# Seven-part products moved from output blocks 2 to 5 to blocks 3 to 6, with all their weight sums on GpSimd

## The chip, the core and the metric

The kernel runs on one core of a Trainium2 chip. The profile calls the engines PE (TensorE, matrix products), DVE (VectorE), ACT (ScalarE), POOL (GpSimd) and SP (SyncE, which issues nearly all transfers from memory). The metric is the device time of one execution in microseconds; a kernel's time is the median of its runs. SBUF is the on-chip memory that engines read and transfers fill, PSUM holds the accumulators of the matrix products in eight banks of 128x512 float32.

## What is computed

One layer of a hybrid encoder for 256 tokens of width 4096: an input projection, two groups of heads, and an output projection with a normalised residual.

```
proj = einsum('bsd,dc->bsc', x, w_in)                  # w_in is 4096 x 16592
fox_out  = forgetting attention over 16 heads of 128
rwkv_out = RWKV-7 delta rule over 32 heads of 64, in chunks, with group norm
h   = concatenate([fox_out, rwkv_out]) * silu(z)
out = einsum('bsc,cd->bsd', h, w_out)                  # 4096 x 4096
x   = layernorm(ALPHA * x + out, ln_gain, ln_bias)
```

The change touches the output projection alone: `h` (256 x 4096) times `w_out` (4096 x 4096).

## The kernel before

**Precision.** Every float32 operand of a large product is split in two parts, a rounded high part and the rest. A product of a 128x128 piece of `h` with a 128x512 piece of weights is then three matmuls: high by high, low by high, high by low (`product`, lines 960, 961 and 963). The weights are split on the way: SP loads a tile of 128x1024 float32 (tag `wr`, four buffers, line 246), ACT writes the high part (line 148, names ending in `h`, four buffers) and DVE subtracts it to give the low part (line 149, names ending in `l`, three buffers). A tile holds two pieces, for two values of the contraction index `k`.

**Blocks and jobs.** The output projection has eight column blocks of 512. The list `plan` sets the order: a plain job `("n", b, q)` takes tile `q` of block `b`, that is `k = 2q` and `2q + 1`, for both halves of the tokens, so 4 products or 12 matmuls. `weights` keeps three jobs split ahead of the PE. Blocks 0 and 1 are done while the heads finish, 6 and 7 are plain.

**Seven-part products.** Blocks 2 and 3, and blocks 4 and 5, are done as pairs. For the six tiles in `FEW` (`q` from 6 to 11) of a pair, the 2 x 2 x 2 = 8 products of two token halves, two `k` and two blocks are replaced by seven (Winograd's form of Strassen's scheme). Call one such `q` a set. It needs sums of the left operand, which are made once for all pairs, and four sums of the weight tiles `one` (block `b`) and `two` (block `b + 1`) for each set:

- `combine_left(q)`: six GpSimd operations (lines 988 to 993) into a tile `sf`. `split_left(q)` then splits it (ACT line 999, DVE line 1000) into `sq` and over half of `h`'s own tile, and starts `combine_left(q + 2)`, since there are two buffers with the tag `t`.
- `combine("e1", b, q)`: GpSimd makes the first half of `ta` (line 277) and the first half of `tb` (line 278), DVE the second half of `ta` (line 281), GpSimd the second half of `tb` (line 282), which still reads tile `one`.

A set is four jobs: `e1` (two products, from tile `one`), `e2` (one, from half of tile `two`), `e3` (two, from `ta`) and `e4` (two, from `tb`), with two plain jobs between them. So a pair is six sets and 20 plain jobs.

**What sets the order around the change.** Each engine takes its instructions in the order in which they stand in its queue, and an instruction that waits holds up all behind it. A scheduler places them by the order of the calls; `tc.issue_after` and `tc.keep_in_program_order` fix some. Work on finished accumulators (`add`, `stats`, `gain`, and `merge` for the shared products) stands in the list `todo`, from which `drain(n)` takes n steps at a job. The left sums' splits of `split_left` stand in the same list. SP's queue holds the weight loads in the order of the jobs; a load waits until its `wr` buffer has been read for the last time.

## Time and profile before

| | |
|---|---|
| median of 3 runs | 1934.72 us (1933.67 to 1937.24) |
| the profiled execution, its own time | 1933.68 us |
| its span in the profile | 1931.9 us |
| PE busy in the span | 1903.4 us |
| block 2 begins on the PE, by the timeline | 1636.63 us |
| first pair ends, second ends, block 6 ends | 1740.72, 1830.44, 1873.96 us |

The kernel's time has 1.8 us outside the span. A matmul of 128x512 shows as about 0.39 us, but a new one begins every 0.23 us, since they overlap; so the PE is read by when matmuls begin and by the idle time ahead of one, not by the sum of their lengths. The rows of the timeline give the start, the duration, the engine, the line, the operation, result and operands, and in brackets the idle time before and what ended it. Tile names in the profile have no numbers of block and buffer: `wo_12l` is the low part of tile 12 of some block, `e_9l` the low part of a sum of set 9, `ta` and `tb` the weight sums, `sf` the left sums.

### The profile page before, as it was taken

What the parts mean: (1) busy time and instruction counts of PE and PEld (TensorE: products, weight loads), DVE (VectorE), ACT (ScalarE), POOL (GpSimd) and SP (SyncE); (2) the same over time, 40 slices, a digit from 0 to 9 for tenths busy, and PEclk for the clock granted to TensorE, in tenths of its full rate; (3) what the DMA queues carried; (4) which work ended last, traced back from release to release, by engine and by line L of the source; (5) the groups of instructions that cost most, each with busy time, mean ns of one, the idle gap of its engine ahead of it and who ended that gap; (6) DMA issues with size and microseconds to landing.
All of it is one profiled execution on the core that took longest, in us unless ns stands there. A gap on an engine that the chain in (4) does not pass through costs nothing.

```text
span 1931.9 us, 28208 instructions
## 1 busy us (share of the span) xinstructions
PE 1903.4 (99%) x9757; PEld 1578.9 (82%) x9757; DVE 1466.6 (76%) x2429; ACT 1007.7 (52%) x1577; POOL 358.8 (19%) x537
## 2 busy tenths in 40 slices
PE   9999999999999999999999999999999999899998
PEld 9887888888888888888888888888888888577786
DVE  7578768776877787678867786778677857789865
ACT  6554565446454645464556455645564555454543
POOL 0012102200220022012101310131013014733200
PEclk9999999999999999999999999999999999999999
DMA  9678766876687668767877787777777877456675
GB/s 345 179 209 227 213 199 220 235 224 193 205 245 221 199 202 253 212 198 219 236 202 214 217 231 200 222 218 223 205 222 224 288 226 229 142 193 211 212 227 182
DMA packets 271459, 421.37 MB, mean 218 GB/s; under 512 B 142482, under 2 KB 171300, under 8 KB 271316
## 3 DMA queue, kind: packets, MB, share of 16 engines
q1 hardware_dynamic: 271028, 419.23, 71.8%
q8 instruction: 76, 1.25, 0.3%
q14 instruction: 67, 0.55, 0.1%
q10 hardware_dynamic: 288, 0.34, 0.1%
HBM read 389.86 MB, written 29.64 MB: 217 GB/s over the span
## 4 chain that ended last, share of the span: by engine, by line
PE 93%; DVE 2%; POOL 2%; DMA 1%; issue 1%; ACT 0%; SPq 0%; DVEq 0%; POOLq 0%; ACTq 0%
PE acc L154 24%; PE acc L156 23%; PE acc L155 23%; PE oacc L963 5%; PE oacc L960 4%; PE oacc L961 4%; PE rh L706 1%; PE gp L592 1%; PE up L737 1%; PE sp L747 1%; PE accl L154 1%; PE accl L155 1%; PE accl L156 1%; DMA wo<-in_w_o_dram 1%; PE yp L769 0%
## 5 line engine op out<-in xcount | busy, mean ns | idle before, releaser
L821 POOL COPY pT<-lg 32x96 f32<-32x96 f32 x128 | 56.1, 438 | 632.9 <-DVE lg L817 628.2
L629 POOL COPY BKt<-BK 32x192 f32<-32x192 f32 x128 | 71.6, 559 | 62.5 <-DVE BK L626 57.5
L662 DVE TENSOR_REDUCE xc<-prod 128x8 f32<-128x16 f32 (+30 forms) x248 | 72.6, 293 | 6.6
L659 DVE TENSOR_TENSOR prod<-Nb,xc 128x8 f32<-128x8 f32 (+30 forms) x248 | 72.3, 291 | 3.0
L149 DVE TENSOR_TENSOR w_0l<-w,w_0h 128x1024 fp32r<-128x1024 f32 x31 | 38.6, 1245 | 37.6 <-ACT w_0h L148 28.5
L148 ACT CAST w_0h<-w 128x1024 fp32r<-128x1024 f32 x31 | 32.5, 1048 | 61.4 <-DMA w<-in_w_main_dram 43.0
L148 ACT CAST w_8h<-w 128x1024 fp32r<-128x1024 f32 x31 | 32.6, 1052 | 47.5 <-DMA w<-in_w_main_dram 21.8
L148 ACT CAST w_6h<-w 128x1024 fp32r<-128x1024 f32 x31 | 32.7, 1055 | 46.9 <-PE acc L155 35.3
L149 DVE TENSOR_TENSOR w_9l<-w,w_9h 128x1024 fp32r<-128x1024 f32 x31 | 38.0, 1225 | 23.0 <-issue 9.6
L149 DVE TENSOR_TENSOR w_11l<-w,w_11h 128x1024 fp32r<-128x1024 f32 x31 | 37.9, 1222 | 21.9 <-PE acc L156 16.2
L149 DVE TENSOR_TENSOR w_10l<-w,w_10h 128x1024 fp32r<-128x1024 f32 x31 | 37.9, 1223 | 19.9 <-PE acc L156 7.3
L149 DVE TENSOR_TENSOR w_15l<-w,w_15h 128x1024 fp32r<-128x1024 f32 x31 | 38.0, 1225 | 19.5 <-issue 16.6
L149 DVE TENSOR_TENSOR w_6l<-w,w_6h 128x1024 fp32r<-128x1024 f32 x31 | 38.9, 1253 | 16.1 <-ACT hry L780 10.3
L518 POOL COPY hr<-hr 32x16 f32<-32x16 f32 x64 | 45.4, 709 | 26.8 <-DVE hr L515 24.4
L154 PE MATMUL acc<-w_15h,x 128*128 128x512 f32 x124 | 50.2, 405 | 0.0
L154 PE MATMUL acc<-w_9h,x 128*128 128x512 f32 x124 | 50.0, 403 | 0.0
L148 ACT CAST w_10h<-w 128x1024 fp32r<-128x1024 f32 x31 | 32.6, 1052 | 32.9 <-DMA w<-in_w_main_dram 19.4
L156 PE MATMUL acc<-w_12l,x 128*128 128x512 f32 x124 | 48.5, 391 | 1.1 <-DVE w_12l L149 1.1
L154 PE MATMUL acc<-w_14h,x 128*128 128x512 f32 x124 | 49.5, 399 | 0.0
L149 DVE TENSOR_TENSOR w_7l<-w,w_7h 128x1024 fp32r<-128x1024 f32 x31 | 37.9, 1221 | 15.1 <-PE acc L156 13.1
L154 PE MATMUL acc<-w_0h,x 128*128 128x512 f32 x124 | 49.1, 396 | 0.0
L154 PE MATMUL acc<-w_1h,x 128*128 128x512 f32 x124 | 49.1, 396 | 0.0
(1058 smaller groups left out, 6821.1 us busy)
## 6 DMA issues: line engine op xcount, KB each, us to landing
w<-in_w_main_dram SPq DMA_DIRECT2D x496, 512.0 KB
wo<-in_w_o_dram SPq DMA_DIRECT2D x128, 512.0 KB
bt<-bk SPq DMA_DIRECT2D x88, 128.0 KB
Nb<-nd SPq DMA_DIRECT2D x16, 512.0 KB
hd<-hl SPq DMA_DIRECT2D x29, 256.0 KB
h<-hd SPq DMA_DIRECT2D x29, 256.0 KB
wr<-in_w_first_dram SPq DMA_DIRECT2D x15, 384.0 KB
lr<-in_w_lora_dram SPq DMA_DIRECT2D x15, 336.0 KB
```

The costliest lines, as they stand in the source:

```text
L148: latest[1] = nc.scalar.copy(hi[:, :n], src[:, :n])
L149: latest[0] = nc.vector.tensor_tensor(lo[:, :n], src[:, :n], hi[:, :n].bitcast(F32), ALU.subtract)
L154: nc.tensor.matmul(acc[:, :n], xs[k][:, 0, tt], hi[:, o : o + n], start=(k == 0), stop=False)
L155: nc.tensor.matmul(acc[:, :n], xs[k][:, 1, tt], hi[:, o : o + n], start=False, stop=False)
L156: nc.tensor.matmul(acc[:, :n], xs[k][:, 0, tt], lo[:, o : o + n], start=False, stop=(k == KT - 1))
L629: nc.gpsimd.tensor_copy(BKt[B * b : B * (b + 1), :, :, B * a : B * (a + 1)], BK[B * a : B * (a + 1), :, : NCH - 1, B * b : B * (b + 1)])
L659: first = nc.vector.tensor_tensor(prod[:, :, :, s + 1 :], nb[:, :, s : s + 1, s + 1 :].to_broadcast([P, 2, NJ, w]), xc[:, :, :, s + 1 :], ...
L662: solved = nc.vector.tensor_reduce(xc[:, :, :, s : s + 1], prod[:, :, :, s:], AX.X, ALU.add)
L821: (nc.gpsimd.tensor_copy if b % 2 else nc.scalar.copy)(pT[B * b : B * (b + 1), :, B * a : B * (a + 1)], lg[B * a : B * (a + 1), :, B * b : ...
L960: nc.tensor.matmul(acc, h, hi, start=n[0] == n[1], stop=False)
L961: nc.tensor.matmul(acc, l, hi, start=False, stop=False)
L963: nc.tensor.matmul(acc, h, lo, start=False, stop=not n[0])
```

## The change

The matmuls are the same in number. What moves:

- **The pairs** are now blocks 3 and 4, and blocks 5 and 6. Block 2 is a plain block between them and block 1, and takes the tiles in `FEW` first, since the left sums overwrite half of those rows of `h`.
- **The left sums.** `combine_left` for the first two sets stays behind block 0. All `split_left` calls, and the `combine_left` calls that they start, stand in `todo` of block 2, of which one step is taken at the jobs with `q` 0, 1, 3, 5 and 13, and one at the first job of block 3.
- **The weight sums** are four GpSimd operations in two jobs of their own, `t12` and `t34`; the DVE operation of line 281 is gone. `t12` comes a plain job and an `e4` earlier than `e1`.
- **Places apart.** The weight tiles of every second set (6, 8 and 10 of each pair) do not use `wr` buffers: `one` goes to a tile with the tag `lr` that is otherwise free, `two` in two halves to the part of `res` that belongs to block 7.
- **Accumulators of blocks 0 and 1** are added, measured and multiplied at once when the block ends, as six DVE operations in a row. Those of block 6 go to `todo`, as do the four `halves` steps, and are taken two at a job in block 7.
- Banks and the places of `load_tok` follow the new pairs.

```diff
-LEAD = (6, 4)
+PAIRS = {3: 3, 4: 3, 5: 5, 6: 5}
+LEAD = 4
...
+    plan += [("n", 2, q) for q in sorted(range(KT // 2), key=lambda q: q not in FEW)]
+    own_place = set()
+    for b in (3, 5):
         plain = [[(n, q) for q in range(KT // 2) if q not in FEW] for n in (b, b + 1)]
...
+        plan += [("n", *t) for t in lead[: LEAD - 2]]
+        for n, q in enumerate(FEW):
+            if n % 2 == 0:
+                own_place.add((b, q))
+            before = units[n - 1][1] if n else lead[-1]
+            plan += [] if n else [("n", *lead[-2])]
+            plan += [("t12", b, q), ("n", *before)] + ([("e4", b, FEW[n - 1])] if n else [])
+            plan += [("t34", b, q), ("e1", b, q), ("n", *units[n][0]), ("e2", b, q), ("e3", b, q)]
+        plan += [("n", *units[-1][1]), ("e4", b, FEW[-1])]
...
     def load():
         name, src = stream.pop()
+        b, q = [int(t) for t in name[2:].split("_")] if name[:2] == "wo" else (0, 0)
+        if b in PAIRS and (PAIRS[b], q) in own_place:
+            if b == PAIRS[b]:
+                raw = const.tile([P, 1024], F32, tag="lr", name=name)
+                nc.sync.dma_start(out=raw, in_=src.rearrange("p k c -> p (k c)"))
...
+            else:
+                apart[name] = [res[j][:, (NB - 1) * OB :] for j in range(2)]
+                for j in range(2):
+                    nc.sync.dma_start(out=apart[name][j], in_=src[:, j, :])
+            return
...
     def combine(kind, b, q):
...
+        g = nc.gpsimd.tensor_tensor
+        if kind[0] == "t":
+            t = sums_of[b, q, kind] = rpool.tile([P, 2 * OB], F32, tag="t", name=f"{kind}_{b}_{q}", bufs=2)
+            if kind == "t12":
+                g(t[:, :OB], b12, b11, ALU.subtract)
+                g(t[:, OB:], b22, t[:, :OB], ALU.subtract)
+            else:
+                g(t[:, :OB], b22, b12, ALU.subtract)
+                g(t[:, OB:], b21, sums_of[b, q, "t12"][:, OB:], ALU.subtract)
+            return
         if kind == "e1":
...
-            nc.gpsimd.tensor_tensor(t12[:, :OB], b12, b11, ALU.subtract)
-            nc.gpsimd.tensor_tensor(t34[:, :OB], b22, b12, ALU.subtract)
-            got = split(raws[one], 2 * OB, one)
-            with tc.issue_after(latest[0].ins):
-                nc.vector.tensor_tensor(t12[:, OB:], b22, t12[:, :OB], ALU.subtract)
-            nc.gpsimd.tensor_tensor(t34[:, OB:], b21, t12[:, OB:], ALU.subtract)
...
     def finished(b):
-        if b > 5:
+        if b < 2:
             with tc.issue_after(latest[0].ins):
-                for m in range(2):
-                    add(m, b)
-                for m in range(2):
-                    gain(m, b)
+                for step in (add, stats, gain):
+                    for m in range(2):
+                        step(m, b)
             return
...
+        if b == NB - 2:
+            todo.append(aggregate)
...
+            drain((2 if n <= LEAD or n > whole else 1) if kind == "n" else kind == "e4")
+        elif b > 1:
+            drain(2 if b == NB - 1 else q in (0, 1, 3, 5, 13))
...
+            if b == 1:
+                todo.extend(lambda q=q: split_left(q) for q in FEW)
+            elif b == 6:
+                todo.extend(lambda n=n: halves(n) for n in range(HALVED))
```

The built programs show the move in three places. The first is DVE's queue around set 8 of the second pair (blocks 4 and 5 before, 5 and 6 now). Before:

```order
L149 TENSOR_TENSOR wo4_8l_16890<-wo4_8_16835,wo4_8h_16889 128x1024
L281 TENSOR_TENSOR ta4_8_16885<-wo5_8_16847,ta4_8_16885 128x512
L1065 TENSOR_TENSOR res0_15796<-res0_15796,lg3_15993 128x512
L149 TENSOR_TENSOR wo4_12l_16911<-wo4_12_16873,wo4_12h_16910 128x1024
L1065 TENSOR_TENSOR res1_15797<-res1_15797,lg3_15993 128x512
L149 TENSOR_TENSOR wo5_8l_16924<-wo5_8_16847,wo5_8h_16923 128x512
L149 TENSOR_TENSOR e3_4_8l_16936<-ta4_8_16885,e3_4_8h_16935 128x1024
L149 TENSOR_TENSOR wo5_2l_16952<-wo5_2_16908,wo5_2h_16951 128x1024
L149 TENSOR_TENSOR e4_4_8l_16961<-tb4_8_16886,e4_4_8h_16960 128x1024
```

and with the change, where `e1`, `e2` and so on are the parts of a set:

```order
L150 TENSOR_TENSOR e1_5_8l_17206<-wo5_8_17122,e1_5_8h_17205 128x1024
L150 TENSOR_TENSOR wo5_12l_17222<-wo5_12_17138,wo5_12h_17221 128x1024
L150 TENSOR_TENSOR e2_5_8l_17234<-res1_15797,e2_5_8h_17233 128x512
L150 TENSOR_TENSOR e3_5_8l_17244<-t12_5_8_17168,e3_5_8h_17243 128x1024
L150 TENSOR_TENSOR wo6_2l_17263<-wo6_2_17231,wo6_2h_17262 128x1024
L150 TENSOR_TENSOR e4_5_8l_17272<-t34_5_8_17202,e4_5_8h_17271 128x1024
```

The sum `ta4_8`, which stood ahead of three splits, is gone from DVE, and so are the two steps of `gain` (L1065) in this set. The second place is SP's queue, the loads of the same sets, with the semaphores that each waits for. Before:

```order
L246 DMA wo4_8_16835<-in_w_o_dram 128x1024 [waits DMAHW5_49,Pool_49]
L937 DMA lg5_16725<-in_lng_dram 128x512 [waits DVE_49]
L246 DMA wo5_8_16847<-in_w_o_dram 128x1024 [waits DMAHW7_49,DMAHW3_49,DVE_49]
L246 DMA wo4_12_16873<-in_w_o_dram 128x1024 [waits DMAHW6_49,DMAHW4_49,DVE_49]
L246 DMA wo5_2_16908<-in_w_o_dram 128x1024 [waits DMAHW0_49,DVE_49]
L246 DMA wo4_9_16921<-in_w_o_dram 128x1024 [waits DMAHW1_49,Pool_49]
L246 DMA wo5_9_16933<-in_w_o_dram 128x1024 [waits DMAHW4_49,DVE_49]
```

and with the change, one set's loads further on:

```order
L266 DMA wo5_12_17138<-in_w_o_dram 128x1024 [waits DMAHW2_49,DVE_49,Pool_49]
L969 DMA lg7_17697<-in_lng_dram 128x512 [waits DMAHW3_49,DVE_49]
L266 DMA wo5_9_17150<-in_w_o_dram 128x1024 [waits DMAHW7_49,DVE_49]
L266 DMA wo6_9_17178<-in_w_o_dram 128x1024 [waits DMAHW5_49,DVE_49]
L365 DMA res0_15796<-in_xtok_dram 128x512 [waits DMAHW6_49]
L365 DMA res1_15797<-in_xtok_dram 128x512
L266 DMA wo6_2_17231<-in_w_o_dram 128x1024 [waits DMAHW1_49,DMAHW0_49,DVE_49]
L263 DMA res0_15796<-in_w_o_dram 128x512 [waits Pool_49]
L257 DMA wo5_10_17300<-in_w_o_dram 128x1024 [waits DMAHW2_49,DVE_49,Pool_49]
L266 DMA wo5_13_17269<-in_w_o_dram 128x1024 [waits DMAHW3_49,DVE_49]
```

Before, the load that waits for POOL is tile `one` of the set that comes next (`wo4_8` waits for set 7's last sum). With the change it is a plain tile that is used behind the next set's `e1` (`wo5_12`, for set 7's last sum) or a tile of a set two further on (`wo5_10`, for set 8's last sum), and tiles `wo5_9` and `wo6_9` stand a full set ahead of their use. The third place is DVE's queue where the left sums are split. Before, between the first jobs of block 2:

```order
L149 TENSOR_TENSOR wo2_2l_15894<-wo2_2_15831,wo2_2h_15893 128x1024
L1000 TENSOR_TENSOR sq6_15897<-sf6_15817,sq6_15897 128x384
L1000 TENSOR_TENSOR h12_14784<-sf6_15817,h12_14784 128x128
L1055 SCALAR_TENSOR_TENSOR res0_15796<-res0_15796,oacc1_0_15418 128x512
L944 TENSOR_SCALAR rt2_15937<-rh2_15935,cs_72 6x512
L149 TENSOR_TENSOR wo2_3l_15925<-wo2_3_15863,wo2_3h_15924 128x1024
L945 SCALAR_TENSOR_TENSOR rows_15798<-rr2_15932,cs_72,rt2_15937 6x512
L1055 SCALAR_TENSOR_TENSOR res1_15797<-res1_15797,oacc1_1_15419 128x512
L1000 TENSOR_TENSOR sq7_15941<-sf7_15824,sq7_15941 128x384
```

and with the change, from the ninth of block 2's 16 jobs on (the tiles 6 to 11 come first):

```order
L150 TENSOR_TENSOR wo2_2l_16004<-wo2_2_15965,wo2_2h_16003 128x1024
L1032 TENSOR_TENSOR sq6_16007<-sf6_15817,sq6_16007 128x384
L1032 TENSOR_TENSOR h12_14784<-sf6_15817,h12_14784 128x128
L976 TENSOR_SCALAR rt3_16300<-rh3_16298,cs_72 6x512
L977 SCALAR_TENSOR_TENSOR rows_15798<-rr3_16295,cs_72,rt3_16300 6x512
L150 TENSOR_TENSOR wo2_3l_16034<-wo2_3_15983,wo2_3h_16033 128x1024
L1032 TENSOR_TENSOR sq7_16037<-sf7_15824,sq7_16037 128x384
L1032 TENSOR_TENSOR h14_14810<-sf7_15824,h14_14810 128x128
L150 TENSOR_TENSOR wo2_4l_16064<-wo2_4_16001,wo2_4h_16063 128x1024
L150 TENSOR_TENSOR wo2_5l_16094<-wo2_5_16031,wo2_5h_16093 128x1024
L1032 TENSOR_TENSOR sq8_16097<-sf8_16012,sq8_16097 128x384
```

The split of `sq6` stood after the third job of the pair that uses it; now it stands seven plain jobs and a lead of four ahead of that pair's first set, and the accumulators of block 1 no longer stand between.

More of the change, by code (lines that the diff above doesn't have):

```diff
@@ L244, in load @@
         name, src = stream.pop()
+        b, q = [int(t) for t in name[2:].split("_")] if name[:2] == "wo" else (0, 0)
[3 more added lines that the diff above has]
+                nc.sync.dma_start(out=raw, in_=src.rearrange("p k c -> p (k c)"))
+                apart[name] = [raw[:, j * OB : (j + 1) * OB] for j in range(2)]
+                apart[name, 0] = raw
+            else:
[3 more added lines that the diff above has]
+            return
         raw = wpool.tile([P, 1024], F32, tag="wr", name=name, bufs=4)
@@ L268, in fetch, with halves_of @@
         ready.append((job, hl[:2], hl[2:]))
+    apart = {}
+    def halves_of(name):
+        while name not in raws and name not in apart:
+            load()
+        if name in apart:
+            return apart[name]
+        return [raws[name][:, j * OB : (j + 1) * OB] for j in range(2)]
     def combine(kind, b, q):
         one, two = f"wo{b}_{q}", f"wo{b + 1}_{q}"
[L272 to L285 removed]
@@ L286, in combine @@
-        if kind == "e2":
-            return split(raws.pop(two)[:, OB:], OB, two)
-        t = sums_of[b, q][kind == "e4"]
-        return split(t, 2 * OB, f"{kind}_{b}_{q}")
+        if kind in ("t12", "t34", "e2"):
+            (b11, b21), (b12, b22) = (halves_of(t) if t == two or kind != "e2" else (None, None) for t in (one, two))
+        g = nc.gpsimd.tensor_tensor
[8 more added lines that the diff above has]
+            return
@@ L291, in weights @@
+        if kind == "e1":
+            t, n = apart.get((one, 0)), 2 * OB
+            t = raws.pop(one) if t is None else t
+        elif kind == "e2":
+            t, n = b22, OB
+            raws.pop(two, None)
+        else:
+            t, n = sums_of[b, q, "t12" if kind == "e3" else "t34"], 2 * OB
+        ready.append(((kind, b, q), *split(t, n, f"{kind}_{b}_{q}")))
     def weights(job):
```

108 lines of the change are left out of this document (49 added, 59 removed).

## The prediction

> **What bounds the kernel now.** I read the page's first part, then busy time by stretch (first pair, second pair, block 6), then what the PE waited for, then the chain of waits, then the timelines of DVE and POOL side by side.
>
> ```profile
> PE 1903.4 (99%) x9757; PEld 1578.9 (82%) x9757; DVE 1466.6 (76%) x2429; ACT 1007.7 (52%) x1577; POOL 358.8 (19%) x537
> ...
> 1636.60:1740.70 104.10, 90.51 (x367) 69.82 (x366) 85.19 (x88) 48.91 (x62) 56.79 (x42) 0.97 0.51 175
> 1740.70:1830.40 89.70, 84.74 (x367) 68.34 (x366) 79.41 (x75) 42.75 (x45) 32.02 (x18) 1.00 0.62 208
> 1830.40:1874.00 43.60, 43.60 (x194) 36.08 (x194) 28.53 (x32) 19.64 (x22) 0.00 (x0) 1.00 0.78 241
> ...
> 1830.44 0.39 PE L960 MATMUL oacc<-wo_0h,h 128*128 128x512 f32 x1
> 1873.96 0.39 PE L960 MATMUL oacc<-wo_0h,h 128*128 128x512 f32 x1
> ```
>
> The columns of a stretch are its length and the busy time of PE, PEld, DVE, ACT and POOL, then granted clock, DMA share and GB/s. The PE is at 99% over the whole span, so what can be won lies where it isn't. Block 6 is plain: 32 values of k, two token halves, three matmuls, so 192 matmuls between the two rows of `wo_0h`, 43.52 us, or 0.2267 us each. A pair has 6 sets of 7 products and 20 plain jobs of 4, 122 products or 366 matmuls, which at that pace take 82.97 us. The first pair took 104.1 us, **21.1 too many**, the second 89.7, **6.7 too many**: 27.8 us in all.
>
> ```profile
> PE oacc L963 <- DVE wo_13l L149: 2.4, 1, 2.4
> ...
> PE oacc L963 <- DVE wo_12l L149: 1.7, 1, 1.7
> ...
> 1659.18 0.63 PE L960 MATMUL oacc<-wo_4h,h 128*128 128x512 f32 x1
> 1659.61 0.63 PE L961 MATMUL oacc<-wo_4h,h 128*128 128x512 f32 x1
> ```
>
> Each wait is for a low part from DVE (the first row is of the first pair, the second of the second). Idle time is 104.1 - 90.5 = 13.6 us in the first pair and 89.7 - 84.7 = 5.0 in the second. The rest is what waits cost afterwards: in the first pair matmuls 0.43 us apart behind the longest waits, at a mean clock of 0.97; in the second 1.7 us over four waits, 0.43 each.
>
> ```profile
> 1693.27 4.59 DMA wo<-in_w_o_dram
> 1698.02 1.90 POOL ta L277
> 1699.94 1.05 DVE ta L281
> ...
> 1703.73 1.22 DVE wo_13l L149
> 1704.99 0.50 PE oacc L963
> ...
> SPq L246 <- POOL tb L282: 79.8, 12, 8.0
> ...
> L281 DVE TENSOR_TENSOR ta<-wo,ta 128x512 f32<-128x512 f32 x12 | 19.1, 1592 | 14.5 <-POOL ta L277 14.5
> L277 POOL TENSOR_TENSOR ta<-wo,wo 128x512 f32<-128x512 f32 x12 | 22.3, 1856 | 71.3 <-DMA wo<-in_w_o_dram 45.5 <-DVE res L1053 18.4 <-DVE wo_8l L149 7.4
> ```
>
> That is a loop. SP's load waits for `tb`, the last reader of tile `one` (12 times, 79.8 us, with all later loads behind it); POOL's `ta` waits for that load (45.5 us); DVE's half of `ta` waits for POOL (14.5 us idle), and the split that the PE needs next, `wo_13l`, stands behind it on DVE.
>
> **The change part by part.**
>
> *The DVE sum goes (-), and the loop with it.* DVE's queue has only splits in a set, each for a sum that POOL was given a whole set earlier. The loads that wait for POOL are now wanted late: by the order, `wo5_12` waits for set 7's last sum and is split after set 8's `e1`.
>
> ```profile
> 1692.52 1.55 SPq L246 DMA_DIRECT2D wo<-in_w_o_dram  x3
> ...
> 1696.23 1.05 ACT L148 CAST wo_9h<-wo 128x1024 fp32r<-128x1024 f32 x1 [1.34 <-DMA wo<-in_w_o_dram]
> ```
>
> From the issue to the cast of the first of three tiles are 3.7 us. Between set 7's last sum and the split of `wo5_12` stand, on DVE, `e2`, `e3`, a plain job, `e4` and `e1`, about 8 us of work by the prices below. So the loads have some 3 us to spare, and I take this term in full: -27.8 us, if nothing takes its place. The two halves of tile `two` cost SP one more issue per second set (0.3 to 0.5 us each by the row above), in a queue that waits far ahead of need: nothing.
>
> *The port that DVE and POOL share (+).*
>
> ```profile
> 1709.94 2.31 DVE L149 TENSOR_TENSOR wo_10l<-wo,wo_10h 128x1024 fp32r<-128x1024 f32 x1
> 1712.18 1.79 DVE L281 TENSOR_TENSOR ta<-wo,ta 128x512 f32<-128x512 f32 x1
> 1713.88 1.21 DVE L149 TENSOR_TENSOR wo_14l<-wo,wo_14h 128x1024 fp32r<-128x1024 f32 x1
> 1715.02 1.78 DVE L149 TENSOR_TENSOR wo_10l<-wo,wo_10h 128x512 fp32r<-128x512 f32 x1
> 1716.73 1.21 DVE L149 TENSOR_TENSOR e_10l<-ta,e_10h 128x1024 fp32r<-128x1024 f32 x1
> ...
> 1709.44 1.73 POOL L277 TENSOR_TENSOR ta<-wo,wo 128x512 f32<-128x512 f32 x1 [6.19 <-DMA wo<-in_w_o_dram]
> 1711.13 2.28 POOL L278 TENSOR_TENSOR tb<-wo 128x512 f32<-128x512 f32 x1
> 1714.04 2.21 POOL L282 TENSOR_TENSOR tb<-wo,ta 128x512 f32<-128x512 f32 x1 [0.63 <-DVE ta L281]
> ...
> L281 DVE TENSOR_TENSOR ta<-wo,ta x12: 691/1768/1786, 1660.2 to 1808.0; 128x512 f32<-128x512 f32 x12
> ...
> L278 POOL TENSOR_TENSOR tb<-wo x12: 1287/1294/2279, 1664.6 to 1807.9; 128x512 f32<-128x512 f32 x12
> ...
> 1752.98 1.05 ACT L148 CAST wo_0h<-wo 128x1024 fp32r<-128x1024 f32 x1 [0.31 <-PE oacc L961]
> ```
>
> Alone, DVE starts a split of 1024 columns every 1.14 us (1713.88 to 1715.02); one of 512 takes 0.60 (691 ns, the least in the row of `ta`, less the 0.08 by which instructions overlap: 1.22 for 1.14). Beside POOL they take 2.31 and 1.78: they take turns, one instruction each. From 1709.94 to 1717.94 DVE did 3 x 1.14 + 2 x 0.60 = 4.62 us of its own in 8.0, with three POOL sums: **1.13 us** for each. A set now asks for 5 x 1.14 + 0.60 = 6.30 of DVE and 4 x 1.13 = 4.52 for POOL, 10.82 us, where the PE needs 15 products x 3 x 0.2267 = 10.20. That is 0.62 us short per set (before: 6.90 + 3.39 = 10.29, which is why the port alone did not bind). POOL's sums for a pair's first set lie in its plain lead, so five sets per pair run short: 3.1 us. Against that stands DVE's lead, least at a plain job behind `e2` and `e3`: its low buffer comes free with the job three before, so the split may end 1.14 us into `e2`, which with `e3` takes 2.04, and the low part is wanted 0.45 after the job begins: 2.04 + 0.45 - 1.14 = 1.35 us. In the second pair two `gain` steps (two inputs in SBUF, 0.60 each) stand late enough in the order to count too. So waits of 3.1 - 1.35 = 1.75 and 3.1 + 1.2 - 1.35 = 2.95 us, at 0.62 a time some 3 and 5 waits, each with 0.43 behind it: 4.7 + 3.4 = **+8.1 us**. Lower bound 0 (POOL finds gaps where DVE waits for buffers), upper bound with POOL's sum in full, below.
>
> *The left sums and the lumps (0).* Six sums of 128 or 256 columns per set move to block 2, and two lumps of six DVE operations stand at the ends of blocks 0 and 1.
>
> ```profile
> 1873.48 1.37 DVE L1055 SCALAR_TENSOR_TENSOR res<-res,oacc 128x512 f32<-128x512 f32 x2 [0.75 <-PE oacc L963]
> 1877.41 1.22 DVE L149 TENSOR_TENSOR wo_2l<-wo,wo_2h 128x1024 fp32r<-128x1024 f32 x1
> ...
> 1638.86 0.74 POOL L988 TENSOR_TENSOR sf<-h 128x256 f32<-128x256 f32 x1 [12.25 <-DVE h L1000]
> ...
> 1642.51 4.72 POOL L990 TENSOR_TENSOR sf<-sf 128x128 f32<-128x128 f32 x1
> ...
> 1648.26 0.74 POOL L988 TENSOR_TENSOR sf<-h 128x256 f32<-128x256 f32 x1
> ...
> 1655.36 2.98 POOL L991 TENSOR_TENSOR sf<-sf 128x128 f32<-128x128 f32 x1
> 1658.42 0.46 POOL L993 TENSOR_TENSOR sf<-sf 128x128 f32<-128x128 f32 x1
> ```
>
> The trace has such a lump, behind block 6: 3.9 us, followed by a split, and no wait in PE's list there. With two plain jobs (5.4 us) split ahead, 3.9 + 1.2 = 5.1 fits. Left sums: three sets took from 1638.86 to 1658.88, 6.7 us each. Four of them from about 1654 end near 1681, when block 3 begins and ten microseconds before its first set. I take 0 for both and 3 us as the upper bound. Block 7 now has two steps at a job, 1.14 + 2 x 0.60 = 2.34 of 2.72 us, for eight of its 16 jobs: hidden under the PE.
>
> *Sum.* 1933.7 - 27.8 + 8.1 = 1914.0 for the profiled execution; the median lies 1.0 above it: **1915 us**. Its own range is 1907 (no new wait) to 1919 (3 us more).
>
> **The rivals.**
>
> *POOL holds the port for its whole instruction.* A sum alone lasts 1.29 us, not the 1.13 that DVE seemed to lose. Then a set asks 6.30 + 5.16 = 11.46, 1.26 short: 6.3 - 1.35 and 7.5 - 1.35 are 11.1 us of waits, with ten restarts of 0.43 15.4: 1934.7 - 27.8 + 15.4 = 1922. For it: the second pair of before, where DVE was busy 79.4 of 89.7 us. Against: the stretch measured above. The Trainium skill speaks for it: "SBUF — State Buffer", section "Who interferes with whom", has the two engines' shared port as an exclusive lock, kept for the whole instruction, taken when DVE has two inputs in SBUF and GpSimd reads SBUF. The trace agrees that they take turns; that the whole 1.29 us counts it does not show.
>
> *Loads still late.* SP still has one POOL wait in each set with loads behind it. If each pair is left with what the second had, 6.7 us, the time is 1934.7 - 27.8 + 13.4 = 1920. For it: the 79.8 us above; against: the tiles that wait are wanted later.
>
> *Block 2 takes the stall.* If a left sum is held off as at 1642.51 in each set (9.4 us from 1638.86 to 1648.26), four end at 1692, 11 us behind the place of the last split; less some 4 us of splits ahead, DVE holds the PE 7 us, and about 2 follow in slow matmuls: 1924.
>
> *Slower: POOL comes too late for `e3` and `e4`.* If DVE's back-to-back splits overtake POOL, as at 1642.51, every `e3` and `e4` waits for a sum and then for its cast, 1.05 us in which neither engine has other work. A set lasts 10.82 + 2.10 = 12.92, 2.72 over the PE's 10.20; ten sets 27.2, twenty restarts 8.6, less 2.7 of lead: 33.1, so 1940. It decides from 28 us on, that is if both waits come in nearly every set; with one per set it is about 18 and still faster. Against: sums of 512 columns in the rows above lost at most one turn.
>
> The Trainium skill speaks against the move itself: "GPSIMD Engine Reference", section "Engine selection", gives elementwise work to VectorE, GpSimd being about twice as slow with two inputs. The trace agrees (0.69 us on DVE at least, 1.29 on POOL), and by that the move would be 12 x 0.6 = 7.2 us lost; in the sum above it is in the 0.62.
>
> **How the numbers follow.** Forecast 0.55, port in full 0.14, loads 0.13, block 2 0.08, POOL late 0.06, and 0.04 that other waits eat it up. The first four are all faster by over 0.2% (3.9 us, about what this measurement can tell): 0.90, less 0.03 for two of them together: 0.87. Slower 0.08, within 0.2% 0.05. The range runs from 1906, no wait at all, to 1926, above block 2's case.
>
> **What would show it.** Right: no DVE wait for POOL sums in front of splits, SP's waits for POOL no longer followed by POOL waiting for DMA, the two pairs 85 to 88 us each, at a clock of 1.00, and block 2 at 43.5. Wrong: POOL idle for DMA in the sets; DVE idle for casts of `t12` or `t34`; PE waits inside block 2; pairs over 92 us; or a stall in block 7.

## The result

| | before | with the change |
|---|---|---|
| median | 1935.53 us (4 runs, 1933.67 to 1937.24) | **1913.45 us** (4 runs, 1912.92 to 1914.28) |
| ratio | | 0.9887, 95% interval 0.9869 to 0.9904 |
| profiled execution: span, own time | 1931.9, 1933.68 us | 1911.1, 1912.92 us |

The forecast was 1915 us, and 1914.0 for the profiled execution. The change made the kernel 1.1% faster. The experiments show that the number came out right while a part of its reasons was wrong.

The profile after, first the page's first part:

```profile
PE 1898.2 (99%) x9757; PEld 1576.5 (82%) x9757; DVE 1477.9 (77%) x2417; ACT 1009.1 (53%) x1577; POOL 404.9 (21%) x549
```

Then busy time by stretch, with the columns as before, for block 2, the pair of blocks 3 and 4, and the pair of blocks 5 and 6:

```profile
1636.60:1681.00 44.40, 43.87 (x193) 35.91 (x192) 33.47 (x41) 21.49 (x31) 25.16 (x24) 1.00 0.66 210
1681.00:1767.50 86.50, 85.26 (x368) 68.13 (x367) 85.03 (x66) 44.77 (x50) 62.05 (x28) 1.00 0.64 217
1767.50:1853.20 85.70, 84.72 (x367) 68.39 (x366) 80.50 (x65) 43.52 (x45) 44.79 (x22) 1.00 0.61 204
```

By the first matmuls of the blocks the pairs take 86.48 and 85.76 us, where they took 104.1 and 89.7, and block 2 takes 44.39 in place of a plain block's 43.52. The clock is 1.00 in both pairs. Block 2 begins at 1636.61, within 0.02 us of before, and block 7 at 1853.24 in place of 1873.96: 20.7 us earlier, and the span is 20.8 shorter. So all of the gain lies between these two points.

What is left of waiting, from the list of what PE waited for:

```profile
PE oacc L995 <- DVE wo_0l L150: 0.8, 1, 0.8
PE oacc L995 <- DVE wo_5l L150: 0.8, 1, 0.8
...
PE oacc L995 <- DVE wo_15l L150: 0.5, 1, 0.5
```

The timeline of PE shows more, in waits too short for that list:

```profile
1715.91 0.50 PE L995 MATMUL oacc<-wo_12l,h 128*128 128x512 f32 x1
1716.24 0.39 PE L992 MATMUL oacc<-wo_12h,h 128*128 128x512 f32 x1
...
1726.60 0.50 PE L995 MATMUL oacc<-wo_13l,h 128*128 128x512 f32 x1
```

The third row of the list is in block 2. At tiles 12, 13, 14 and 15 of the first pair the matmul with the low part starts 0.48 to 0.50 us behind the one ahead of it instead of 0.23, and the next one 0.33 behind that. From one such place to the next it is 10.69 us: a set with its two plain jobs now takes that. The timeline of DVE over one set says why:

```profile
1713.53 2.32 DVE L150 TENSOR_TENSOR wo_12l<-wo,wo_12h 128x1024 fp32r<-128x1024 f32 x1
1715.78 1.78 DVE L150 TENSOR_TENSOR e_8l<-res,e_8h 128x512 fp32r<-128x512 f32 x1
1717.48 1.21 DVE L150 TENSOR_TENSOR e_8l<-t,e_8h 128x1024 fp32r<-128x1024 f32 x1
1718.61 1.21 DVE L150 TENSOR_TENSOR wo_2l<-wo,wo_2h 128x1024 fp32r<-128x1024 f32 x1
1719.75 2.32 DVE L150 TENSOR_TENSOR e_8l<-t,e_8h 128x1024 fp32r<-128x1024 f32 x1
1721.99 2.31 DVE L150 TENSOR_TENSOR e_9l<-wo,e_9h 128x1024 fp32r<-128x1024 f32 x1
1724.23 2.32 DVE L150 TENSOR_TENSOR wo_13l<-wo,wo_13h 128x1024 fp32r<-128x1024 f32 x1
```

From 1713.53 to 1724.23 DVE has not one idle moment. It does five splits of 1024 columns and one of 512, 6.30 us by itself, and four of them last 1.1 us too long, one for each POOL sum: 10.70 us.

The loop of before is gone. SP still waits for POOL, and POOL no longer waits for a load; these are rows of the lists for SP and POOL in the two pairs:

```profile
SPq L263 <- POOL t L310: 24.9, 5, 7.1
SPq L266 <- POOL t L311: 19.6, 6, 3.4
...
POOL t L307 <- issue: 18.4, 9, 3.0
```

No row of POOL's list names a DMA, where before it had 45.5 us of them.

### The profile page after: what moved, and what is told of

Its sections match the earlier page's. It is cut to its first block, busy times and chain, and to the rows that moved or that the text cites. A ratio compares the mean times of both kernels' runs of the same rounds, so it can differ in the third digit from the quotient of the medians.

```text
span 1911.1 us, 28218 instructions
## 1 busy us (share of the span) xinstructions
PE 1898.2 (99%) x9757; PEld 1576.5 (82%) x9757; DVE 1477.9 (77%) x2417; ACT 1009.1 (53%) x1577; POOL 404.9 (21%) x549
## 4 chain that ended last, share of the span: by engine, by line
PE 95%; DVE 2%; POOL 1%; DMA 1%; ACT 0%; issue 0%; SPq 0%; DVEq 0%; ACTq 0%; POOLq 0%
PE acc L155 24%; PE acc L157 24%; PE acc L156 24%; PE oacc L995 5%; PE oacc L992 5%; PE oacc L993 5%; PE rh L738 1%; PE gp L624 1%; PE up L769 1%; PE sp L779 1%; PE accl L157 0%; PE p L993 0%; PE accl L156 0%; PE p L995 0%; PE p L992 0%; PE accl L155 0%
## 5 line engine op out<-in xcount | busy, mean ns | idle before, releaser
L150 DVE TENSOR_TENSOR w_0l<-w,w_0h 128x1024 fp32r<-128x1024 f32 x31 | 38.4, 1238 | 33.6 <-ACT w_0h L149 25.1
L150 DVE TENSOR_TENSOR w_9l<-w,w_9h 128x1024 fp32r<-128x1024 f32 x31 | 38.0, 1226 | 24.7 <-ACT w_9h L149 9.8
L150 DVE TENSOR_TENSOR w_11l<-w,w_11h 128x1024 fp32r<-128x1024 f32 x31 | 37.9, 1223 | 21.8 <-PE acc L157 16.1
L150 DVE TENSOR_TENSOR w_10l<-w,w_10h 128x1024 fp32r<-128x1024 f32 x31 | 37.9, 1223 | 20.4 <-issue 7.9
L150 DVE TENSOR_TENSOR w_15l<-w,w_15h 128x1024 fp32r<-128x1024 f32 x31 | 38.0, 1225 | 18.3 <-issue 12.9
L150 DVE TENSOR_TENSOR w_6l<-w,w_6h 128x1024 fp32r<-128x1024 f32 x31 | 38.9, 1255 | 16.0 <-ACT hry L812 10.3
L149 ACT CAST w_1h<-w 128x1024 fp32r<-128x1024 f32 x31 | 32.7, 1053 | 33.9 <-DMA w<-in_w_main_dram 21.3
L150 DVE TENSOR_TENSOR w_7l<-w,w_7h 128x1024 fp32r<-128x1024 f32 x31 | 37.9, 1222 | 15.1 <-PE acc L157 13.1
L150 DVE TENSOR_TENSOR w_3l<-w,w_3h 128x1024 fp32r<-128x1024 f32 x31 | 37.8, 1221 | 14.9 <-PE acc L157 14.6
```

Of the source, the lines that this page charges most:

```text
L149: latest[1] = nc.scalar.copy(hi[:, :n], src[:, :n])
L150: latest[0] = nc.vector.tensor_tensor(lo[:, :n], src[:, :n], hi[:, :n].bitcast(F32), ALU.subtract)
```

## The experiments

The question was which part of the change made the 27.8 us of excess go, and what the four POOL sums cost. The kernels below are named by their number; the quoted expectations have the number with a longer name. Times in different groups of runs are compared by their ratio to the kernel before, which had medians of 1932.9 to 1935.5 us in these groups, and where a few microseconds matter, by the length of the two pairs in the profiles. The table is a summary; "pairs" are measured from the first matmul of the pair's first block to that of the block behind it.

| kernel | left sums | places apart | weight sums made by | pairs, us | median, us | ratio (95%) |
|---|---|---|---|---|---|---|
| before | in first pair | no | POOL 3, DVE 1, in `e1` | 104.1, 89.7 | 1932.9 to 1935.5 | 1 |
| e10 | in first pair | yes | as before | 102.65, 85.7 | 1928.75 | 0.9971 (0.9959 to 0.9983) |
| e5 | in first pair | no | as before | 102.0, 90.2 | 1931.55 | 0.9994 (0.9985 to 1.0003) |
| e1 | in block 2 | no | as before | 90.5, 90.4 | 1922.23 | 0.9940 (0.9924 to 0.9956) |
| e7 | in block 2 | yes | as before | 84.95, 84.3 | 1910.26 | 0.9882 (0.9865 to 0.9898) |
| e2 | in block 2 | no | POOL 4, in jobs | 100.9, 99.9 | 1942.15 | 1.0041 (1.0025 to 1.0057) |
| e11 | in block 2 | yes | POOL 4, in `e1` | 87.4, 85.8 | 1912.92 | 0.9886 (0.9870 to 0.9903) |
| changed | in block 2 | yes | POOL 4, in jobs | 86.5, 85.8 | 1913.45 | 0.9887 (0.9869 to 0.9904) |
| e3 | in block 2 | yes | POOL 5, in jobs | 94.1, 90.0 | 1924.49 | 0.9953 (0.9935 to 0.9971) |
| e4 | in block 2 | yes | POOL 3, DVE 1, in jobs | 85.1, 84.8 | 1910.88 | 0.9879 (0.9863 to 0.9895) |
| e6 | as e4, gains later | yes | as e4 | 84.0, 84.0 | **1908.83** | 0.9876 (0.9861 to 0.9890) |
| e8 | as e7, gains later | yes | as before | 84.0, 83.6 | 1909.52 | 0.9870 (0.9855 to 0.9885) |
| e9 | as e6 | yes | POOL 2, DVE 2, in jobs | 83.6, 83.6 | 1909.51 | 0.9867 (0.9851 to 0.9884) |

### e1: the old weight sums in the new layout

```diff
-            plan += [("t12", b, q), ("n", *before)] + ([("e4", b, FEW[n - 1])] if n else [])
-            plan += [("t34", b, q), ("e1", b, q), ...
+            plan += [("n", *before)] + ([("e4", b, FEW[n - 1])] if n else [])
+            plan += [("e1", b, q), ...
...
+        if kind == "e1":
+            ...
+            g(t12[:, :OB], b12, b11, ALU.subtract)
+            g(t34[:, :OB], b22, b12, ALU.subtract)
+            ready.append(((kind, b, q), *split(raws[one], 2 * OB, f"{kind}_{b}_{q}")))
+            with tc.issue_after(latest[0].ins):
+                nc.vector.tensor_tensor(t12[:, OB:], b22, t12[:, :OB], ALU.subtract)
+            g(t34[:, OB:], b21, t12[:, OB:], ALU.subtract)
```

> The changed kernel with the weight sums made as before: no jobs t12 and t34, no places apart; POOL's ta and tb, then DVE's half of ta behind the split of e1, then POOL's last half, all in e1. Pairs, block 2 and left sums stay as changed. Theory (the loop of load, POOL sum and DVE sum is what cost both pairs): each pair is again at least 6.7 us over its 82.97, as the second pair was, where no left sums stood: 1913.5 - 6.3 + 13.4 = 1921 at least, POOL waits for DMA again (over 30 us in the pairs) and DVE's half of ta waits for POOL (over 10 us). Up to 1934 if the loop alone made the first pair's 21.1. Rival (what cost the first pair was the left sums among the weight sums, and moving them to block 2 is the gain): not over 1916.

Measured: 1922.23 us. The stretches of its two pairs:

```profile
1681.40:1771.90 90.50, 85.12 (x367) 68.28 (x367) 77.76 (x72) 44.05 (x49) 32.96 (x19) 1.00 0.60 209
1771.90:1862.40 90.50, 85.42 (x368) 68.22 (x367) 77.81 (x70) 42.88 (x46) 32.43 (x18) 1.00 0.61 204
```

and its waits:

```profile
DVE t L308 <- POOL t L304: 13.8, 11, 1.9
...
POOL t L304 <- DMA wo<-in_w_o_dram: 65.7, 11, 7.3
...
SPq L264 <- POOL t L309: 88.4, 12, 8.3
```

The loop is back in full, with the same three rows as before, and each pair is 7.5 us over its 82.97. Both pairs are now alike: with the same sums and loads as before, the first pair is 13.6 us shorter than it was. So the loop never cost 27.8 us; about half of that is something else that the change took out of the first pair.

### e5: the left sums back in the first pair

```diff
-            drain(2 if b == NB - 1 else q in (0, 1, 3, 5, 13))
+            drain(2 if b == NB - 1 else 0)
...
-            if b == 1:
-                todo.extend(lambda q=q: split_left(q) for q in FEW)
+            if b == 2:
+                a, d, g1 = todo[:2], todo[2:4], todo[4:]
+                parts = [[], a, [], d, g1, []]
+                todo[:] = [f for q, before in zip(FEW, parts) for f in (*before, lambda q=q: split_left(q))]
```

> e1_old_sums (old weight sums, pairs in blocks 3 to 6) with the left sums put back among the first pair's own work: no steps are taken in block 2; split_left of the six sets and block 2's adds, stats and gains stand in todo in the order that the kernel before has for them, two steps at each of the four lead jobs, one at each plain job of the sets. Theory (in the first pair the left sums, on POOL's queue ahead of the weight sums, made 90.5 into 104.1): first pair 101 to 106 us, block 2 at 43.5, the second pair unchanged at 90.4: 1922.2 + 13.6 - 0.9 = 1935 (1931 to 1938). Rival (the 13.6 us came from the accumulators of blocks 0 and 1, whose 12 steps stood in the first pair before and still stand at the ends of those blocks here, or from the lead): first pair at most 95 us, 1926 or less.

Measured: 1931.55 us, within the theory's range. Of its stretches, the first pair:

```profile
1681.30:1783.30 102.00, 90.03 (x368) 69.53 (x367) 82.15 (x80) 46.41 (x57) 53.80 (x42) 0.97 0.52 178
```

and a piece of its chain of waits, with the start, the length and what it was:

```profile
1702.19 1.05 POOL sf L1016
...
1713.68 0.45 POOL sf L1021
1714.13 1.23 POOL t L304
1715.38 0.70 DVE t L308
1716.16 1.05 ACT e_7h L149
1717.24 0.68 DVE e_7l L150
```

Twelve left-sum operations for two sets stand on POOL's queue ahead of set 7's first weight sum and take it from 1702.19 to 1714.13, 11.9 us. The sum, DVE's half, the cast and the split follow one behind the other, and PE stands idle for 4.0 us at the cast of `e_7h`. It is the order on POOL's queue, and not the work, that costs this: the same operations in block 2 lengthen block 2 by 0.9 us (44.38 us in e1, 43.52 here without them). The first pair of the kernel before is 2.1 us longer still than e5's; that is left to the accumulators of blocks 0 and 1 and the rest of the layout, which no run separates.

### e10: the places apart alone, in the kernel before

```diff
     def load():
         name, src = stream.pop()
+        b, q = [int(t) for t in name[2:].split("_")] if name[:2] == "wo" else (0, 0)
+        if b in (2, 3, 4, 5) and q in FEW[::2]:
+            if b % 2 == 0:
+                raw = const.tile([P, 1024], F32, tag="lr", name=name)
+                ...
+            else:
+                apart[name] = [res[j][:, (NB - 1) * OB :] for j in range(2)]
+                ...
+            return
```

> The kernel before with one part of the change: the weight tiles of sets 6, 8 and 10 of both pairs (blocks 2 to 5) in places apart, all else as it was. Theory (the late load is the loop's cause in both pairs, as e7 against e1 showed 12 us for two pairs): second pair 84 to 86 us in place of 89.7, first pair 97 to 101 in place of 104.1 with the left sums still in it, POOL's waits for DMA under 20 us in place of 45.5; 1923 (1920 to 1926). Rival (in the first pair POOL is late by the left sums alone, so early loads change nothing there): 1928 to 1931.

Measured: 1928.75 us, which is the rival's number. Its two pairs:

```profile
1636.80:1739.40 102.60, 92.20 (x367) 72.10 (x366) 86.62 (x88) 49.17 (x61) 59.18 (x43) 0.93 0.57 183
1739.40:1825.20 85.80, 84.46 (x368) 68.38 (x367) 81.75 (x75) 43.56 (x46) 32.38 (x17) 1.00 0.64 205
```

In the second pair early loads are worth 4.0 us, as the theory said. In the first they are worth 1.4 only, where the theory had 3 to 7. POOL's list in that pair no longer names a DMA (22.9 us before), so the tiles are there, and POOL is late by the left sums all the same. PE's idle time there fell by 3.2 us (13.6 to 10.4), but more of its matmuls were slow, at a mean granted clock of 0.93 in place of 0.97, and that took back the rest. The two causes lie side by side in the first pair: taking out the left sums alone brings about 11.5 to 13.6 us (e5 or before against e1), early loads alone 1.4, and both 19.1 (before against e7).

### e7 and e11: places apart with the sums still made in `e1`

e7 is e1 with the places apart of the changed kernel:

```diff
+            if n % 2 == 0:
+                own_place.add((b, q))
...
+            raw = apart.get((one, 0))
+            raw = raws.pop(one) if raw is None else raw
```

> e1_old_sums with the places apart of the changed kernel for sets 6, 8 and 10, so the sums are still made in e1 by POOL, DVE, POOL, but every second set's tiles are loaded early and no longer stand behind a POOL sum of the set just before. Theory (the late load is what delays POOL and through it DVE; the sum itself costs DVE only 1.3 to 1.9 us of waiting): POOL's waits for DMA in the pairs under 25 us in place of 65.7, pairs of 86 to 88 us, 1914 to 1918. Rival (sums made in e1 are too late for DVE whatever the load does, so jobs of their own are needed): pairs stay at 90, 1920 to 1923.

Measured: 1910.26 us, better than the theory. Its pairs are 3.0 us shorter than those of the changed kernel; the two ratios to the kernel before lie closer together, with intervals that overlap. Its stretches and the first row of what POOL waited for:

```profile
1681.50:1766.40 84.90, 84.49 (x367) 68.23 (x366) 82.81 (x72) 44.98 (x50) 41.19 (x21) 1.00 0.65 220
1766.40:1850.80 84.40, 83.94 (x368) 68.68 (x367) 78.23 (x70) 43.67 (x46) 30.06 (x16) 1.00 0.61 207
```

```profile
POOL t L313 <- DVE t L312: 16.5, 12, 7.7
```

POOL's 65.7 us of waiting for DMA are gone altogether, and so are DVE's 13.8 us of waiting for POOL, though half of the sets still use `wr` buffers and DVE still makes its half of `ta` in `e1`. I had expected DVE to go on waiting 1.3 to 1.9 us for each sum; with the tiles early POOL has the sum done by then. So the loop is broken by the early loads alone: the two pairs are 11.6 us shorter in e7 than in e1.

e11 puts all four sums on POOL, without jobs of their own:

```diff
             g(t12[:, :OB], b12, b11, ALU.subtract)
+            g(t12[:, OB:], b22, t12[:, :OB], ALU.subtract)
             g(t34[:, :OB], b22, b12, ALU.subtract)
+            g(t34[:, OB:], b21, t12[:, OB:], ALU.subtract)
...
-                nc.vector.tensor_tensor(t12[:, OB:], b22, t12[:, :OB], ALU.subtract)
```

> e7_old_sums_places with all four weight sums by POOL, made one behind the other in e1 (t12, then t34), so the changed kernel without the jobs t12 and t34. Theory (with the loads early, jobs of their own are worth nothing; a fourth POOL sum costs 0.25 to 0.4 us a set by the port): 1912.5 to 1914.5, sets of 10.7 us from tile to tile. Rival (four POOL sums at 2.2 us beside DVE last 8.8 us and come too late for e4 when they begin in e1, so jobs of their own are what all sums on POOL need): DVE idle for the casts of t34, 1916 or more.

Measured: 1912.92 us, the changed kernel's time. The jobs `t12` and `t34`, which make the sums a plain job and an `e4` earlier, bring nothing that the runs can tell, with the sums by POOL (e11 against the changed kernel) or with DVE's half (e7 against e4).

### e2: the jobs and the POOL sums without places apart

```diff
-            if n % 2 == 0:
-                own_place.add((b, q))
```

> The changed kernel without places apart: the weight tiles of all sets go through the four wr buffers. Theory: t12 asks for both tiles of a set while the tiles of two plain jobs are in the buffers too, so that all four are taken and each load waits for a split or a POOL sum of the set just before, some 4.6 us ahead of the next sum; POOL waits for DMA again, 1918 to 1930. Rival (that the sums stand in jobs of their own is enough, SP's waits were never late): 1912 to 1915.

Measured: 1942.15 us, above the theory's range and slower than before. The mechanism is the one expected, of a larger size. A piece of its chain of waits:

```profile
1723.57 0.69 DVE e_8l L150
1724.26 4.55 DMA wo<-in_w_o_dram
...
1728.91 1.05 ACT wo_2h L149
...
1729.99 1.44 DVE wo_2l L150
...
1731.47 0.50 PE oacc L993
```

With both tiles of the next set asked for early, all four buffers are taken, and the plain tile behind `e3` gets the one that the split of `e2` has just left. It needs a load of 4.55 us, a cast and a split, where PE has the rest of a plain tile and three products to do in between, some 4 us; it then stands idle for 1.68 us at the cast and 0.73 at the split. So the early sums, all on POOL and without the places, make the kernel slower by 20 us than the old ones (e2 against e1), and it is the places apart that they rest on.

### e3 and e4: one POOL sum more, one POOL sum less

e3 makes the first half of `t34` twice:

```diff
                 g(t[:, :OB], b22, b12, ALU.subtract)
+                g(t[:, :OB], b22, b12, ALU.subtract)
```

> The changed kernel with POOL's first half of t34 made twice, so five POOL sums of 512 columns per set in place of four; nothing else differs. Theory (in the sets DVE is never idle and each POOL sum takes a turn of about 1.10 us from it): a set from wait to wait lasts 10.69 + 1.10 = 11.79 us, ten bound sets 11 us in all: 1924.5 (1923 to 1927). With POOL's whole 1.29 us counted: 12.0 us per set, 1927. Rival (the short waits that are left come from the latency of a sum or a load, POOL having 2 to 3 us idle in each set): 1913 to 1916.

Measured: 1924.49 us, against 1924.5 expected. Two waits of PE in its timeline, at the same place of two sets that follow each other:

```profile
1743.28 0.50 PE L996 MATMUL oacc<-wo_14l,h 128*128 128x512 f32 x1 [0.59 <-DVE wo_14l L150]
1755.06 0.50 PE L996 MATMUL oacc<-wo_15l,hl 128*128 128x512 f32 x1 [0.58 <-DVE wo_15l L150]
```

They lie 11.78 us apart, where the changed kernel has 10.69. A POOL sum of 512 columns thus takes 1.10 us from DVE, less than the 1.29 that it lasts alone.

e4 gives the second half of `t12` back to DVE:

```diff
-                g(t[:, OB:], b22, t[:, :OB], ALU.subtract)
             else:
                 g(t[:, :OB], b22, b12, ALU.subtract)
+                s = sums_of[b, q, "t12"]
+                with tc.issue_after(latest[0].ins):
+                    nc.vector.tensor_tensor(s[:, OB:], b22, s[:, :OB], ALU.subtract)
```

> The changed kernel with the second half of t12 made by DVE again, in job t34, ahead of the split of e1; the other three sums by POOL. Theory (port): a set asks 6.30 + 0.60 + 3 x 1.10 = 10.20 us, what the PE takes, so the short waits at tiles 12 to 15 go (0.37 us each, seven of them, 2.5 us): 1911 (1909.5 to 1912.5). Rival (a DVE instruction that waits for a POOL sum costs more than the turn it saves, as 14.5 us of DVE idle in the kernel before): DVE idle for POOL t12 over 5 us in the pairs, 1916 or more.

Measured: 1910.88 us (1910.71 to 1911.05), with 1911 expected. All that is left of PE's waiting in the pairs is one row of its list:

```profile
PE oacc L997 <- DVE wo_5l L150: 0.9, 2, 0.6
```

A set takes 10.44 us from tile 13 to tile 14, and DVE waits for no sum. Moving the fourth sum to POOL thus lost 2.4 us in the pairs (172.24 against 169.88), and 3.9 between e7 and e11.

### e6, e8 and e9: what is left

The waits at tiles 0 and 5 stand where the pair's first sets meet the steps that are left of the block ahead. In the changed kernel's timeline of DVE:

```profile
1690.88 1.60 DVE L1099 TENSOR_TENSOR res<-res,lg 128x512 f32<-128x512 f32 x1
...
1693.54 1.77 DVE L1099 TENSOR_TENSOR res<-res,lg 128x512 f32<-128x512 f32 x1
...
1697.34 2.22 DVE L150 TENSOR_TENSOR wo_0l<-wo,wo_0h 128x1024 fp32r<-128x1024 f32 x1 [0.29 <-ACT wo_0h L149]
```

Two `gain` steps, held to 1.60 and 1.77 us by POOL's sums beside them, stand ahead of the split that PE then waits for. e6 is e4 with the gains of blocks 2 and 4 behind the sets of the next pair:

```diff
-                (behind if step is not add else todo).append(lambda step=step, m=m: step(m, b))
-        if b not in (3, 5):
+                (behind if step is gain and b in (2, 4) else todo).append(lambda step=step, m=m: step(m, b))
+        if b in (3, 5):
             todo.extend(behind)
             behind.clear()
```

> e4_dve_sum with the two gain steps of block 2, and of block 4, moved from the lead of the next pair behind that pair's sets, where a plain job leaves DVE 1.6 us free. Theory (the wait at tile 5 in the first two sets, 0.59 and 0.27 us idle with what follows it, is DVE late by those steps, which took 1.6 and 1.8 us beside POOL): both waits go, 1909.4 (1908.8 to 1910.2). Rival (the wait comes from the sets themselves, when sums and splits begin to share the port): 1910.5 to 1911.2.

Measured: 1908.83 us, and both waits are gone. The pairs are 1.9 us shorter than e4's, but the span is only 1.1 shorter (1907.9 against 1909.0), since 0.7 us came back behind them: two more steps stand at the start of block 7, and PE's list there has a new row, `PE oacc L997 <- DVE wo_15l L150: 0.4, 1, 0.4`. From block 7's first matmul to the end of the span it is 58.6 us in e6, 59.2 in e8 and 58.9 in e9, where e4 and e7 have 57.9. That the later steps make this wait was not tested. e8 makes the same edit in e7:

> e7_old_sums_places (sums made in e1 by POOL, DVE, POOL; places apart) with the gain steps of blocks 2 and 4 behind the sets, as in e6_late_gains. Theory (jobs of their own for the sums are worth nothing once the loads are early): the same as e6_late_gains, 1908.8, within 0.8 us; the waits at tiles 4 and 5 go (0.41 and 0.46 us idle). Rival (the early sums give slack that counts when the gains no longer stand in the lead): 1909.8 or more.

Measured: 1909.52 us, within 0.8 of e6, as expected of jobs that are worth nothing. e9 gives DVE a second sum, behind the split of `e1`:

```diff
-                g(t[:, OB:], b21, sums_of[b, q, "t12"][:, OB:], ALU.subtract)
...
+        if kind == "e1":
+            with tc.issue_after(latest[0].ins):
+                nc.vector.tensor_tensor(sums_of[b, q, "t34"][:, OB:], ..., sums_of[b, q, "t12"][:, OB:], ALU.subtract)
```

> e6_late_gains with the second half of t34 made by DVE too, behind the split of e1, so two POOL sums and two DVE sums in a set. Theory (port: a set asks 6.30 + 2 x 0.60 + 2 x 1.10 = 9.70 us in place of 10.20, so DVE gets ahead of the PE): a set from tile to tile takes 10.2 to 10.3 us in place of 10.44, ten sets, 1906.8 (1906.3 to 1907.8). Rival (10.44 is what the PE itself takes in a set): 1908.4 to 1909.2. Rival (DVE waits for POOL's first half of t34, which begins only behind the split of e4): over 5 us of DVE idle for it, 1909.5 or more.

Measured: 1909.51 us (1908.13 to 1910.95), where 1906.8 was expected. The stretches of its pairs:

```profile
1683.00:1766.60 83.60, 83.60 (x367) 68.73 (x367) 73.53 (x76) 45.06 (x50) 25.88 (x15) 1.00 0.72 223
1766.60:1850.20 83.60, 83.60 (x367) 68.73 (x366) 73.85 (x78) 43.59 (x45) 14.84 (x10) 1.00 0.65 208
```

A set takes 10.30 us, as the theory said, and PE is never idle in the pairs: they are as short as this PE order can be. But that is 0.8 us less than e6 for both pairs, and its profiled execution came to block 3 1.8 us later than e6's (1683.05 against 1681.24), from work far ahead of the change. What makes that stretch vary stays open. e6, e8 and e9 can't be told apart. Each is faster than before; against the changed kernel their pairs are 4.2 to 5.1 us shorter, but the intervals of the ratios overlap with its own.

## Why the prediction was right, and where it was not

**The number came out partly by luck.** Redone for the profiled execution with what was measured, the sum is 1933.7 - 27.8 + 6.3 in the pairs + 0.9 in block 2 = 1913.1, and the run took 1912.92. But the forecast gave the 27.8 to the wrong edit, and the edit that it took as nothing was needed: without it, in e2, the kernel takes 1942 us.

**"The DVE sum goes, and the loop with it": the old excess went nearly as forecast, the cause was wrong.** The loop was read rightly from the rows, but I credited its end to the edit that removes one of its members, DVE's sum. e7 keeps that sum in its old place and has no loop; e11 and the changed kernel have it on POOL, and their pairs are 3.9 and 3.0 us longer. What broke the loop are the loads of every second set in places apart, which I had costed as "nothing" in one sentence about SP's queue. The spare 3 us for the loads that I worked out exist only with these places: e2 shows what comes without them.

**"The left sums and the lumps (0)" failed as a cost of zero that hid a gain.** I asked only what the left sums would cost in block 2. What they did in the first pair I had put into the loop's account, since the rows there name the same engines. Half of the first pair's 21.1 us were theirs: 11.5 us by e5 against e1. The row in the prediction that showed it was the left-sum operation of 4.72 us at 1642.51, with POOL going on with left sums until 1658.88; I used it for the cost in block 2 and not to ask what stood behind it on POOL's queue. In block 2 the cost is 0.9 us. It reaches DVE by a row step of `load_tok`, which waits for its cast, and that cast stands on ACT behind the cast of a left sum:

```profile
1674.47 0.52 ACT L1031 CAST sq<-sf 128x384 fp32r<-128x384 f32 x1 [3.61 <-POOL sf L1025]
...
1675.09 0.62 ACT L974 CAST rh<-rr 6x512 fp32r<-6x512 f32 x1
...
1675.74 0.80 DVE L976 TENSOR_SCALAR rt<-rh,cs 6x512 f32<-6x512 f32 x1 [2.16 <-ACT rh L974]
```

The left sum was late because one operation of it lasted 3.73 us beside DVE's splits, as at 1642.51 before. DVE stood idle for 2.16 us, and the split of `wo_15l` came late behind it. In e5, where block 2 has the row steps but no left sums, DVE does not wait for such a cast and block 2 takes 43.52 us.

**The port was right in kind; what a wait costs was misread.** Forecast 8.1 us of new excess over 82.97 a pair, measured 3.51 + 2.79 = 6.3. A POOL sum takes 1.10 us from DVE (1.13 forecast), and a set 10.69 (10.82 forecast). PE's own time for a set is 10.30 by e9 and not 10.20, since the products of a set begin 0.229 us apart; so the shortfall is 0.4 us per set and not 0.62, and 0.6 us of each pair's excess is no wait at all. The waits were nearly as many as forecast (5 and 4, with 3 and 5 forecast), but a short one at tiles 12 to 15 costs 0.37 us in all, 0.26 ahead of the matmul that waits and 0.11 behind it, where the forecast had 0.62 and 0.43. The 0.43 was the second pair's 1.7 us that are not idle time, over its four waits. Some 0.7 of that is the same slower pace of PE. At each wait 0.16 us more lies in the profile itself, which lets a matmul end 0.39 us after its start where the next could begin after 0.23. Behind the wait there too only one matmul is late, by 0.11 us:

```profile
1777.71 0.50 PE L963 MATMUL oacc<-wo_12l,h 128*128 128x512 f32 x1 [1.67 <-DVE wo_12l L149]
1778.05 0.39 PE L960 MATMUL oacc<-wo_12h,h 128*128 128x512 f32 x1
```

What I had not counted are the two longer waits from the gains, which e6 removed.

**The rivals.** *POOL holds the port for its whole instruction* is refuted as a price: 1.10 us per sum, and 1.29 would have made e3's sets 12.0 us. The Trainium skill, "SBUF — State Buffer", section "Who interferes with whom", states an exclusive lock; the timelines agree that the two engines take turns, one instruction each, and the price measured here is lower than the sum's own length. *Loads still late* is not what the change left, but it is what the change would have had without the places apart. *Block 2 takes the stall* came true in kind, by a held-off left sum, but cost 0.9 us and not 9. *POOL too late for `e3` and `e4`* did not come up: DVE's list of waits in the pairs names no cast of a weight sum, though one cast, in the first set, waited 2.2 us for POOL. The move of the sum from DVE to POOL cost 2.4 us in the pairs; that the "GPSIMD Engine Reference" of the Trainium skill (section "Engine selection") speaks against such a move was right, and in the sum above it had been seen and outweighed by a gain that belonged to another edit.

## What to carry to other kernels

Where a change has several parts and the profile one loop, do not credit the loop's end to the part that removes a member of it; ask for each part alone what the loop would do, above all for the part that seems to be only storage. A late load is cured by a place to put it: earlier use of the same four buffers, with one sum more on POOL, made the kernel slower by 20 us. And an engine's queue that holds two kinds of work (here left sums and weight sums) is to be read for what stands behind each, before the waits are put down to either. Work moved off a full engine gains nothing if the other engine takes the same port for longer: 1.10 us taken to save 0.60.

## What the runs showed of the hardware

- DVE and POOL, both busy with two-input sums from SBUF, take strict turns: a DVE split of 1024 columns lasts 2.32 us beside a POOL sum where it lasts 1.21 alone, and each POOL sum of 512 columns costs DVE 1.10 us, by e3 against the changed kernel (11.78 against 10.69 us a set).
- Behind a single wait one matmul is late by 0.11 us (0.34 in place of 0.23), whether the wait was short (0.1 us idle in the changed kernel) or long (1.67 us before, 2.06 in e1). A stretch of matmuls 0.43 us apart is another matter. In e2 it followed on two waits of 1.83 and 0.74 us that came close together and lasted 5.1 us, at a granted clock of 0.50; its timeline of PE, and the stretch:

```profile
1743.44 0.50 PE L990 MATMUL oacc<-wo_3h,h 128*128 128x512 f32 x1 [1.83 <-ACT wo_3h L149]
...
1744.92 0.79 PE L993 MATMUL oacc<-wo_3l,h 128*128 128x512 f32 x1 [0.74 <-DVE wo_3l L150]
1745.51 0.63 PE L990 MATMUL oacc<-wo_3h,h 128*128 128x512 f32 x1
...
1745.50:1750.60 5.10, 5.10 (x13) 3.95 (x12) 2.59 (x3) 1.35 (x2) 3.42 (x2) 0.50 0.42 110
```

  In e10 a single wait of 2.05 us was followed by such a stretch of 3.0 us, so the length of a wait alone does not tell which it will be.
  The Trainium skill, "TensorE: Matmul & The Clock Gate", section "Part 1: The HAM clock gate", has a matmul of 512 columns start every 426.7 ns while the clock is halved, after an idle window of some 3.4 us. The 0.43 us agrees; the waits ahead of it were shorter here.
- 45 matmuls of a set take 10.30 us with no wait in them, 0.229 each, against 0.2267 in plain blocks.
